# A two-layer transformer trunk on one core: first SwiGLU begun with its 256-column part, x loaded later, and one product order for all down parts

## The chip, the cores and the metric

The kernel runs on one core of a Trainium2 chip. The core has a matrix engine (PE), a vector engine (DVE), an activation engine (ACT), a general engine (POOL) and a sync engine (SP) that issues DMAs. Each engine takes its instructions in the order in which they were queued and waits on semaphores for the others. The metric is device time in microseconds for one execution of the whole program, and the median of several runs is compared.

## What is computed

Two layers, each with a SwiGLU, a token mixer (eight forgetting-attention heads and four differential-attention heads) and a second SwiGLU, all with residuals; then a final RMSNorm. There are 512 tokens, width 1024, inner width 2816, and everything is float32. What matters here is the SwiGLU and the norm at the end:

```python
def _rmsnorm(x, gain):
    x32 = x.astype(jnp.float32)
    y = x32 * lax.rsqrt(jnp.mean(x32 * x32, axis=-1, keepdims=True) + NORM_EPS)
    return (y * gain.astype(jnp.float32)).astype(x.dtype)

def _swiglu(h, w_gate_up, w_down):
    g, u = jnp.split(h @ w_gate_up, 2, axis=-1)
    return (jax.nn.silu(g) * u) @ w_down
...
  x = x + 1/2 * SwiGLU_1(RMSNorm(x))
  x = x + W_out [FoX_heads(h) ; Diff_heads(h)],  h = RMSNorm(x)
  x = x + 1/2 * SwiGLU_2(RMSNorm(x))
```

## The kernel before

**Arithmetic.** Every float32 matmul is three matmuls of a rounded type (`mm3`, lines 389 to 391: high by high, high by low, low by high). So every operand has a high part (a cast by ACT, line 85) and a low part (a subtraction by DVE, line 86). A weight tile is 128 x 1024 (512 KB), is cast into a ring of five slots, and is asked for four units ahead (`ensure`, `next_w`).

**Parts.** A SwiGLU is cut along its 2816 inner columns into six parts (`CHUNKS`): five of 512 and one of 256, the third. Each part has a gate-and-up step ("u") and a down step ("d"); the order is u0, u1, d0, u2, d1, ..., u5, d4, d5. The text calls d5 the last down part.

**Products.** Each step is a 2 x 2 block product done with seven products in place of eight, named "1" to "7". The weight of a product is a block (11, 12, 21, 22) or a sum. "5" (21+22) and "7" (11+21) are made by a load of one block (SP) and an accumulate-DMA of the other onto it (POOL, line 136). The sum for "6" is added by DVE (line 147) from block 11 and the one of "5", and the sum for "3" by DVE (line 151) from block 12 and that of "6". A u product on a 512-column part has 24 matmuls of 512 columns in two weight units; on the 256-column part it has 24 matmuls of 256 columns and one weight unit. A down product has 12 matmuls of 512 columns (6 on the 256-column part). The order of products is `STEADY` = 1562734, except `FIRST` = 1256374 in u0 and `FINAL` = 1265734 in d5. In the first two products of u0 the two token halves are interleaved.

**The forms of x.** Products need x in seven forms (`XFORM`): the blocks of x for "1", "2", "3" and sums for the rest. At the start of the program they are made from the transposed x (`xT`, loaded by line 1204, into `xin`): block forms of the first token half (line 368 and the casts), then `first_forms` (lines 374 to 384) for the second half and the sums, partly on ACT, mostly on DVE; `ws` is their scratch, and the tiles `xf` hold the result.

**Start.** PE runs 18 warm-up matmuls (line 264). `first_rms` sums the squares of xT (ACT 1233, DVE 1235, PE 1238) and the reciprocal root `nst` (line 315) is needed by the silu of part 0 (line 445). `load_x` (line 1243) loads x in its untransposed form, four times 512 KB, which the first down step adds to; `first_consts` loads constants.

**Down steps and hooks.** The results of a down step are added to x by DVE (`upd`, line 515), four [128 x 512] pieces per product pair. PSUM has eight banks; tag "b" has five, tag "a" three. In a down step, a pair of accumulators (`pa`, tag b) is used by products 1, 6, 7 and 4 in turn, another pair of tag b by product 2, and a pair of tag a by 5 and 3. After each product of d5 a hook runs: `to_next` begins the next stage (after "6" the first half of the tokens, k-pairs 0 and 1, is transposed by PE, line 327, and split into the tiles XA by ACT 343 and DVE 344), and in the last SwiGLU `tail` prepares the final norm (POOL multiplies by the gain, line 1143).

Of the kernel before, what the change touches and what calls it, by code (L numbers as in the profile page):

```python
# [46 lines left out]
FINAL = "1265734"  # L47
# [7 lines left out]
def trunk(ctx, tc, xT, x, gains, gain_row, w_gu, w_dn, w_in, w_ff, w_out, fbias, lams, subln, consts, rope, out):  # L55
# [358 lines left out]
    def gate_up(c, order, after):  # L414

        cols = CHUNKS[c]
        units = 2 if cols == 512 else 1
# [12 lines left out]
        def done(q, p):  # L430
            rc, nr = norm["rc"], norm["nr"]
# [114 lines left out]
    def ffn(pieces, x_done):  # L546
# [3 lines left out]
        def turned(c):  # L550
            yf[c] = []
            fs = turn_h(c, hs.pop(c), (("X", 2), ("X", 3)) if c == NCH - 1 else ("y0", "y1"), yf[c])
# [617 lines left out]
    def to_next(prep, first, q):  # L1170
# [182 lines left out]
```

## Time and profile before

| what | value |
|---|---|
| runs before | 1898.7, 1898.39, 1896.07 us |
| median | 1898.39 us |
| profiled execution, its own time | 1896.68 us |
| its span in the trace | 1894.8 us |
| PE busy | 1836.0 us (97% of the span) |
| DVE busy | 1623.8 us (86%) |
| ACT busy | 1142.4 us (60%) |
| granted clock, mean | 0.987 of full |

The profiled execution was 1.7 us quicker than the median, and its span leaves out 1.9 us of its time. PE is busy in nearly all of the span. The places to read are the few where it is not, and those where its granted clock is below 1.00.

### The profile page before, as it was taken

How to read it: one execution, taken by the hardware profiler on the slowest of the kernel's cores; microseconds unless marked ns; L12 is line 12 of the kernel's file. 1: busy time of each engine (PE TensorE's matmuls, PEld its weight loads, DVE VectorE, ACT ScalarE, POOL GpSimd, SP SyncE). 2: the span in 40 equal slices, each digit the busy share in tenths (PEclk: the TensorE clock that was granted, in tenths of full speed). 3: DMA queues.
4: the chain of work that ended last, by engine and by line, in shares of the span. 5: the costliest groups of instructions: out<-in, count | busy, mean ns of one | idle time of the engine just before them, and what ended most of it. 6: DMA issues, size and time to landing. Idle time of an engine off the chain costs nothing.

```text
span 1894.8 us, 24754 instructions
## 1 busy us (share of the span) xinstructions
PE 1836.0 (97%) x8814; PEld 1508.7 (80%) x8814; DVE 1623.8 (86%) x2538; ACT 1142.4 (60%) x1800; POOL 128.6 (7%) x156
## 2 busy tenths in 40 slices
PE   5999999899999999999999999999999999999997
PEld 2888888687877889888778988877788788888885
DVE  7789898978685989899998989997786869998998
ACT  5646556555786755565486556555677957455564
POOL 1000000000000000000001000000000000000101
PEclk7999999999999999999999999999999999999999
DMA  9675675243346576676558666552433367756742
GB/s 293 179 213 148 188 213 151 80 123 112 96 123 194 158 194 177 158 212 181 165 141 234 167 173 181 174 142 95 129 101 108 108 177 198 207 146 187 221 116 85
DMA packets 96107, 305.39 MB, mean 161 GB/s; under 512 B 12632, under 2 KB 15192, under 8 KB 95984
## 3 DMA queue, kind: packets, MB, share of 16 engines
q1 hardware_dynamic: 75104, 232.68, 36.6%
q0 software_dynamic: 19584, 69.21, 20.7%
q10 hardware_dynamic: 1296, 1.93, 0.4%
q8 instruction: 69, 1.13, 0.2%
q14 instruction: 54, 0.44, 0.1%
HBM read 289.03 MB, written 2.16 MB: 154 GB/s over the span
## 4 chain that ended last, share of the span: by engine, by line
PE 82%; DVE 8%; ACT 5%; DMA 2%; issue 1%; SPq 0%; POOL 0%; DVEq 0%; ACTq 0%
PE ps_c L389 12%; PE ps_c L390 12%; PE ps_c L391 11%; PE ps L391 9%; PE ps L389 9%; PE ps L390 9%; PE ps_a L389 3%; PE ps_a L390 3%; PE ps_a L391 3%; DVE wg L86 2%; PE ps_t L486 2%; DVE x L515 2%; DMA raw<-w_gu 1%; PE ps_a L661 1%; PE ps_a L662 1%; PE ps_a L663 1%
## 5 line engine op out<-in xcount | busy, mean ns | idle before, releaser
L85 ACT CAST wg<-raw 128x1024 fp32r<-128x1024 f32 (+1 forms) x534 | 544.7, 1028 | 507.8 <-PE ps L391 178.3
L86 DVE TENSOR_TENSOR wg<-raw,wg 128x1024 fp32r<-128x1024 f32 (+1 forms) x534 | 629.0, 1187 | 119.8 <-ACT wg L85 117.9
L389 PE MATMUL ps_c<-wg,xf 128*128 128x512 f32 (+1 forms) x768 | 287.8, 375 | 19.6 <-ACT wg L85 18.8
L390 PE MATMUL ps_c<-wg,xf 128*128 128x512 f32 (+1 forms) x768 | 286.6, 373 | 4.4 <-DVE wg L86 4.4
L391 PE MATMUL ps_c<-wg,xf 128*128 128x512 f32 (+1 forms) x768 | 285.5, 373 | 0.0
L389 PE MATMUL ps<-wg,xf 128*128 128x512 f32 (+1 forms) x576 | 218.3, 379 | 0.5 <-ACT wg L85 0.5
L390 PE MATMUL ps<-wg,xf 128*128 128x512 f32 (+1 forms) x576 | 214.9, 373 | 0.0
L391 PE MATMUL ps<-wg,xf 128*128 128x512 f32 (+1 forms) x576 | 214.4, 373 | 0.0
L389 PEld LDWEIGHTS ps_c<-wg,xf 128*128 128x128 f32 x768 | 144.9, 189 | 48.3 <-ACT wg L85 20.5
L390 PEld LDWEIGHTS ps_c<-wg,xf 128*128 128x128 f32 x768 | 144.9, 189 | 30.6 <-DVE wg L86 5.9
L391 PEld LDWEIGHTS ps_c<-wg,xf 128*128 128x128 f32 x768 | 145.1, 189 | 25.6 <-DVE xf L86 0.5
L136 POOL DMA_DIRECT2D raw<-w_gu x88 | 76.4, 868 | 1145.7 <-DMA raw<-w_gu 682.6
L389 PE MATMUL ps_c<-wg,hf 128*128 128x512 f32 x352 | 139.2, 396 | 2.4 <-DVE x L515 2.1
L391 PE MATMUL ps_c<-wg,hf 128*128 128x512 f32 x352 | 137.7, 391 | 0.0
L390 PE MATMUL ps_c<-wg,hf 128*128 128x512 f32 x352 | 137.6, 391 | 0.0
L515 DVE SCALAR_TENSOR_TENSOR x<-ps_c,x 128x512 f32<-128x512 f32 x192 | 123.7, 679 | 2.1 <-PE ps_c L391 2.0
L389 PEld LDWEIGHTS ps<-wg,xf 128*128 128x128 f32 x576 | 109.2, 190 | 19.5 <-ACT wg L85 1.4
L391 PEld LDWEIGHTS ps<-wg,xf 128*128 128x128 f32 x576 | 109.0, 189 | 19.2
L390 PEld LDWEIGHTS ps<-wg,xf 128*128 128x128 f32 x576 | 109.3, 190 | 17.9 <-DVE wg L86 0.2
L389 PE MATMUL ps<-wg,hf 128*128 128x512 f32 x264 | 103.7, 394 | 8.1 <-DVE x L515 8.1
L389 PE MATMUL ps_a<-XA,wg 128*128 128x512 f32 x256 | 106.0, 414 | 2.6 <-ACT XA L343 2.6
L390 PE MATMUL ps<-wg,hf 128*128 128x512 f32 x264 | 103.9, 393 | 1.4 <-DVE wg L86 1.4
(275 smaller groups left out, 3514.2 us busy)
## 6 DMA issues: line engine op xcount, KB each, us to landing
raw<-w_gu SPq DMA_DIRECT2D x218, 512.0 KB, 4.6
raw<-w_dn SPq DMA_DIRECT2D x100, 512.0 KB, 3.4
raw<-w_gu POOLq DMA_DIRECT2D x88, 512.0 KB, 7.0
raw<-w_in SPq DMA_DIRECT2D x48, 512.0 KB, 3.5
raw<-w_dn POOLq DMA_DIRECT2D x40, 512.0 KB, 5.5
kdup<-qk_t SPq DMA_DIRECT2D x64, 128.0 KB, 2.4
raw<-w_out SPq DMA_DIRECT2D x16, 512.0 KB, 3.5
raw<-w_dn SPq DMA_DIRECT2D x20, 256.0 KB, 3.2
```

Source lines behind the costliest of these rows:

```text
L85: act.copy(out=hi, in_=src)
L86: dve.tensor_tensor(out=lo, in0=src, in1=rf(hi), op=ALU.subtract)
L136: pool.dma_start(out=t, in_=where(two, h)[1], accum_op=ALU.add)
L389: pe.matmul(p, lh, rh, start=start, stop=False, skip_group_check=again)
L390: pe.matmul(p, lh, rl, start=False, stop=False, skip_group_check=again)
L391: pe.matmul(p, ll, rh, start=False, stop=stop, skip_group_check=again)
L486: pe.transpose(pj[j][:, e * 256 + p * P:e * 256 + (p + 1) * P], hs[j][p][:, o:o + P], ident)
L515: dve.scalar_tensor_tensor(out=xc, in0=src, scalar=scale, in1=xc, op0=ALU.mult, op1=ALU.add)
L661: pe.matmul(pv[t], xh[:, ts], wh[:, sl], start=k == 0, stop=False)
L662: pe.matmul(pv[t], xh[:, ts], wl[:, sl], start=False, stop=False)
L663: pe.matmul(pv[t], xl[:, ts], wh[:, sl], start=False, stop=k == KT - 1)
```

## The change

The first SwiGLU of layer 0 alone is cut as (256, 512, 512, 512, 512, 512); the other three keep their cut. So u0 there has products of 24 half-width matmuls with one weight unit each. The host packs the weights to match. In this u0 the finishing of product "2", which needs the reciprocal root, is done after "6". At the start all four loads of the first token half of xT come ahead of the second weight, and the weight for "2" comes as one load; the loads behind are asked for earlier than the constants; `first_rms` moves from behind product 2 to behind the third product. `load_x` keeps its place in the list of pieces, 6, but u0 now has seven units, so the four loads of x come after the last of them and behind the weight loads asked for until then. `FINAL` is gone: d5 takes `STEADY`, in all four SwiGLUs, and the hooks of product 6 move to 7; in `tail` those of 7 move to 3.

```diff
-CHUNKS = (512, 512, 256, 512, 512, 512)
-COL0 = [sum(CHUNKS[:i]) for i in range(len(CHUNKS))]
+PARTS_OF = [(256, 512, 512, 512, 512, 512)] + [(512, 512, 256, 512, 512, 512)] * (2 * DEPTH - 1)
...
 STEADY = "1562734"
 FIRST = "1256374"
-FINAL = "1265734"
...
     def part_order(kind, c):
-        if kind == "u":
-            return FIRST if c == 0 else STEADY
-        return FINAL if c == NCH - 1 else STEADY
+        return FIRST if (kind, c) == ("u", 0) else STEADY
...
         def done(q, p):
-            rc, nr = norm["rc"], norm["nr"]
...
+            late = {"2": "", "6": "62"} if first and c == 0 else {}
+            for r in late.get(q, q):
+                done_one(r, p)
...
+        def done_one(q, p):
+            rc, nr = norm.get("rc"), norm.get("nr")
...
-        elif q == "6":
+        elif q == "7":
...
                 early_half(t, 0)
-        elif q == "7":
+        elif q == "3":
...
                 early_half(t, 1)
-        elif q == "3":
...
                 sq(t, 0)
...
-        elif q == "6":
+        elif q == "7":
...
                 prep(0, kp, None)
         elif q == "3":
...
     load_xt(0, 0)
     step[0] = 512
     ensure(1)
-    load_xt(0, 1)
+    for kp in range(1, KP):
+        load_xt(0, kp)
+    step[0] = 1024
...
-    step[0] = 1024
-    for kp in (0, 1):
-        prep_forms(0, 0, kp, xf[:, kp, :, 0:256])
-    load_xt(0, 2)
-    load_xt(0, 3)
-    ensure(4)
-    for kp in (2, 3):
+    for kp in range(KP):
         prep_forms(0, 0, kp, xf[:, kp, :, 0:256])
     for kp in range(KP):
         load_xt(1, kp)
+    running.append(True)
+    ensure(3)
...
-    running.append(True)
...
         for kp in kps:
             prep_forms(0, 1, kp, xf[:, kp, :, 256:512])
...
-        acc = t_tile([P, S], F32, "acc", 5)
+        acc = home("y1", [P, S], F32, "acc")
...
     def load_x():
...
-    pieces = {0: [lambda: first_forms((0, 1))], 1: [lambda: first_forms((2, 3)), first_rms], 6: [load_x]}
+    pieces = {0: [lambda: first_forms((0, 1))], 1: [lambda: first_forms((2, 3))], 2: [first_rms], 6: [load_x]}
...
-        ffn(pieces, lambda q, l=l: to_next(plain_, lambda: mixer_loads(l), q))
+        ffn(2 * l, pieces, lambda q, l=l: to_next(plain_, lambda: mixer_loads(l), q))
```

**DVE at the start.** The names: `raw` are loaded weight blocks, `wg` split weights, `xf` the forms. First as it was, from the sums for the last pairs of x on:

```order
L383 SCALAR_TENSOR_TENSOR ws_251<-ws_251 128x256
L86 TENSOR_TENSOR xf2_158<-ws_251,xf2_158 128x512
L384 SCALAR_TENSOR_TENSOR ws_251<-ws_251,bt_155 128x256
L375 SCALAR_TENSOR_TENSOR ws_261<-xin_109,ngains_70,bt_162 128x256
L376 SCALAR_TENSOR_TENSOR ws_261<-xin_109,ngains_70,ws_261 128x256
L383 SCALAR_TENSOR_TENSOR ws_261<-ws_261 128x256
L86 TENSOR_TENSOR xf2_159<-ws_251,xf2_159 128x768
L86 TENSOR_TENSOR wg_190<-raw_187,wg_190 128x1024
L384 SCALAR_TENSOR_TENSOR ws_261<-ws_261,bt_162 128x256
L86 TENSOR_TENSOR wg_236<-raw_193,wg_236 128x1024
L86 TENSOR_TENSOR xf3_165<-ws_261,xf3_165 128x512
L86 TENSOR_TENSOR xf3_166<-ws_261,xf3_166 128x768
```

and now, from the first block sum on:

```order
L145 TENSOR_TENSOR raw_112<-raw_160,raw_112 128x1024
L84 TENSOR_TENSOR wg_163<-raw_160,wg_163 128x1024
L149 TENSOR_TENSOR raw_123<-raw_123,raw_112 128x1024
L84 TENSOR_TENSOR wg_191<-raw_112,wg_191 128x1024
L84 TENSOR_TENSOR xf1_139<-ws_241,xf1_139 128x768
L84 TENSOR_TENSOR wg_200<-raw_123,wg_200 128x1024
L84 TENSOR_TENSOR wg_253<-raw_166,wg_253 128x1024
L372 SCALAR_TENSOR_TENSOR ws_280<-xin_109,ngains_70,ws_280 128x256
L379 SCALAR_TENSOR_TENSOR ws_280<-ws_280 128x256
L84 TENSOR_TENSOR xf2_145<-ws_280,xf2_145 128x512
L380 SCALAR_TENSOR_TENSOR ws_280<-ws_280,bt_142 128x256
L371 SCALAR_TENSOR_TENSOR ws_290<-xin_109,ngains_70,bt_149 128x256
```

The sums of blocks (now line 145, 149) and four weight low parts stand ahead of the forms of the third and fourth k-pair (`xf2`, `xf3`), where they stood behind them.

**ACT at the end of u0.** The table load that follows `nst` belongs to silu; `p1` and `u2` are its operands. As it was:

```order
L315 ACT_TABLE_LOAD
L315 ACTIVATE nst_299<-nst_299 128x4
L85 CAST wg_379<-raw_150 128x1024
L445 ACT_TABLE_LOAD
L445 ACTIVATE p1_321<-p1_321,nst_299 128x512
L445 ACTIVATE p1_329<-p1_329,nst_299 128x512
```

and now:

```order
L311 ACT_TABLE_LOAD
L311 ACTIVATE nst_364<-nst_364 128x4
L83 CAST wg_513<-raw_195 128x1024
L83 CAST wg_529<-raw_171 128x1024
L446 ACT_TABLE_LOAD
L446 ACTIVATE p1_215<-p1_215,nst_364 128x256
L446 ACTIVATE p1_229<-p1_229,nst_364 128x256
L451 ACTIVATE u2_393<-u2_393,nst_364 128x256
L451 ACTIVATE u2_409<-u2_409,nst_364 128x256
```

Two casts of weights of u1 (`wg_513`, `wg_529`) stand between the reciprocal root and the table load for silu, where there was one, of u0's product 4 (`wg_379`). The first of the two takes a ring slot that product 4 of u0 frees.

**DVE at the change from d4 to d5, first SwiGLU.** `upd` is line 515 before, 516 now; `ps_c` are the pairs of pa, `ps_5` and `ps_2` those of products 5/3 and 2. As it was:

```order
L147 TENSOR_TENSOR raw_2567<-raw_2548,raw_2567 128x1024
L515 SCALAR_TENSOR_TENSOR x2_107<-ps_5_2605,x2_107 128x512
L151 TENSOR_TENSOR raw_2610<-raw_2610,raw_2567 128x1024
L86 TENSOR_TENSOR wg_2734<-raw_2567,wg_2734 128x1024
L515 SCALAR_TENSOR_TENSOR x3_108<-ps_5_2606,x3_108 128x512
L86 TENSOR_TENSOR wg_2752<-raw_2548,wg_2752 128x1024
L515 SCALAR_TENSOR_TENSOR x0_105<-ps_c_2583,x0_105 128x512
L515 SCALAR_TENSOR_TENSOR x1_106<-ps_c_2584,x1_106 128x512
L86 TENSOR_TENSOR wg_2771<-raw_2588,wg_2771 128x1024
L515 SCALAR_TENSOR_TENSOR x0_105<-ps_c_2769,x0_105 128x512
L515 SCALAR_TENSOR_TENSOR x1_106<-ps_c_2770,x1_106 128x512
```

and now:

```order
L145 TENSOR_TENSOR raw_2564<-raw_2545,raw_2564 128x1024
L516 SCALAR_TENSOR_TENSOR x2_107<-ps_5_2602,x2_107 128x512
L516 SCALAR_TENSOR_TENSOR x3_108<-ps_5_2603,x3_108 128x512
L84 TENSOR_TENSOR wg_2731<-raw_2564,wg_2731 128x1024
L84 TENSOR_TENSOR wg_2748<-raw_2607,wg_2748 128x1024
L516 SCALAR_TENSOR_TENSOR x0_105<-ps_c_2580,x0_105 128x512
L149 TENSOR_TENSOR raw_2607<-raw_2607,raw_2564 128x1024
L516 SCALAR_TENSOR_TENSOR x1_106<-ps_c_2581,x1_106 128x512
L84 TENSOR_TENSOR wg_2768<-raw_2585,wg_2768 128x1024
L516 SCALAR_TENSOR_TENSOR x0_105<-ps_c_2766,x0_105 128x512
L516 SCALAR_TENSOR_TENSOR x1_106<-ps_c_2767,x1_106 128x512
```

Here `ps_c_2583` (now 2580) is the accumulator of d4's product 4, `ps_5_2605` (now 2602) that of its product 3, and `ps_c_2769` (now 2766) that of d5's product 1. The two updates from product 3 stand together now, ahead of two weight low parts; the sum of line 149 stands between the two from product 4.

## Rows read from the trace of the kernel before

**Rows 1.** The page: busy time of each engine, its share of the span, instructions.
```profile
PE 1836.0 (97%) x8814; PEld 1508.7 (80%) x8814; DVE 1623.8 (86%) x2538; ACT 1142.4 (60%) x1800; POOL 128.6 (7%) x156
```

**Rows 2.** Windows of the start, and of one half-width product; clock stands before DMA share.
```profile
core 0: us, PE busy (x) PEld busy (x) DVE busy (x) ACT busy (x) POOL busy (x), PEclk, DMA share, GB/s
0.00:15.00 15.00, 13.72 (x45) 6.74 (x45) 6.43 (x10) 11.51 (x22) 1.35 (x11) 1.00 0.88 288
15.00:24.00 9.00, 5.10 (x22) 3.86 (x21) 9.00 (x18) 6.73 (x13) 4.70 (x7) 0.98 1.03 355
24.00:46.00 22.00, 4.15 (x8) 2.13 (x8) 17.08 (x23) 10.17 (x13) 0.85 (x1) 0.50 1.01 276
46.00:54.00 8.00, 8.00 (x23) 6.66 (x24) 4.07 (x12) 2.07 (x3) 0.86 (x1) 0.50 0.88 259
55.00:60.00 5.00, 5.00 (x24) 4.14 (x23) 1.23 (x1) 4.97 (x8) 0.00 (x0) 1.00 0.61 163
...
135.60:138.47 2.87, 2.87 (x25) 2.86 (x24) 2.87 (x4) 1.43 (x2) 0.86 (x1) 1.00 0.40 60
```

**Rows 3.** PE's timeline: start, duration, instruction, idle time before it with its releaser.
```profile
38.33 0.79 PE L389 MATMUL ps_c<-wg,xf 128*128 128x512 f32 x1 [18.23 <-ACT wg L85]
...
45.94 0.80 PE L390 MATMUL ps_c<-wg,xf 128*128 128x512 f32 x1 [1.60 <-DVE wg L86]
```

**Rows 4.** Timelines of SP and POOL: loads of x, and the first accumulate-DMA.
```profile
17.39 1.54 SPq L1243 DMA_DIRECT2D x<-x  x3
...
18.53 1.05 POOL L136 DMA_DIRECT2D raw<-w_gu  x1 [0.98 <-DMA raw<-w_gu]
```

**Rows 5.** ACT's timeline: the cast that awaits the first accumulated block, then the end of part 0.
```profile
27.89 1.04 ACT L85 CAST wg<-raw 128x1024 fp32r<-128x1024 f32 x1 [2.74 <-DMA raw<-w_gu]
...
55.52 1.28 ACT L445 ACT_TABLE_LOAD   x1
56.81 1.34 ACT L445 ACTIVATE p<-p,nst 128x512 f32<-128x512 f32 x2
```

**Rows 6.** DVE's timeline, the start: form steps, a block sum (weight low parts last as long).
```profile
24.61 0.47 DVE L376 SCALAR_TENSOR_TENSOR ws<-xin,ngains,ws 128x256 f32<-128x256 f32 x1
...
25.34 0.94 DVE L86 TENSOR_TENSOR xf<-ws,xf 128x768 fp32r<-128x768 f32 x1
...
35.98 1.22 DVE L147 TENSOR_TENSOR raw<-raw 128x1024 f32<-128x1024 f32 x1
```

**Rows 7.** The page's groups with waits in down steps, and the first such wait (PE's timeline).
```profile
L389 PE MATMUL ps_c<-wg,hf 128*128 128x512 f32 x352 | 139.2, 396 | 2.4 <-DVE x L515 2.1
...
L389 PE MATMUL ps<-wg,hf 128*128 128x512 f32 x264 | 103.7, 394 | 8.1 <-DVE x L515 8.1
...
L390 PE MATMUL ps<-wg,hf 128*128 128x512 f32 x264 | 103.9, 393 | 1.4 <-DVE wg L86 1.4
...
352.88 0.50 PE L389 MATMUL ps<-wg,hf 128*128 128x512 f32 x1 [3.01 <-DVE x L515]
```

**Rows 8.** Windows of the first wait, and behind the second and third; columns as Rows 2.
```profile
350.00:355.00 5.00, 1.65 (x6) 1.05 (x6) 5.00 (x7) 1.38 (x3) 0.00 (x0) 1.00 0.00 0
942.00:944.00 2.00, 2.00 (x6) 1.24 (x5) 2.00 (x3) 0.00 (x0) 0.00 (x0) 0.50 0.60 231
944.00:946.00 2.00, 2.00 (x7) 1.59 (x8) 2.00 (x4) 1.05 (x1) 0.86 (x1) 0.69 0.75 262
1280.00:1282.00 2.00, 1.67 (x4) 0.88 (x4) 2.00 (x4) 1.05 (x1) 0.00 (x0) 0.50 0.31 66
```

**Rows 9.** The first mixer's start: a split of XA (ACT), and PE's first projection.
```profile
359.30 0.83 ACT L343 ACTIVATE XA<-ps_t,gains_sb 128x256 fp32r<-128x256 f32 x2
...
372.59 0.50 PE L389 MATMUL ps_a<-XA,wg 128*128 128x512 f32 x1 [0.68 <-ACT XA L343]
```

**Rows 10.** The page, DMA issues: KB each, median us from issue to landing.
```profile
raw<-w_gu POOLq DMA_DIRECT2D x88, 512.0 KB, 7.0
...
raw<-w_dn POOLq DMA_DIRECT2D x40, 512.0 KB, 5.5
```

More of the change, by code (lines that the diff above doesn't have):

```diff
@@ L164, in gu_units @@
     def gu_units(n, c, order, i):
-        groups = 2 if CHUNKS[c] == 512 else 1
-        base = sum(8 if w == 512 else 4 for w in CHUNKS[:c])
+        groups = PARTS_OF[n][c] // 256
+        base = sum(8 if w == 512 else 4 for w in PARTS_OF[n][:c])
         tags = {("11", 0): "R0", ("11", 1): "R1", ("7", 0): "R2", ("22", 0): "V0", ("7", 1): "V1",
@@ L172, in dn_units @@
     def dn_units(n, c, order, i):
-        cols = CHUNKS[c] // 256 * 512
-        base = sum(CHUNKS[:c]) // 256 * 4 * 512
+        cols = PARTS_OF[n][c] // 256 * 512
+        base = sum(PARTS_OF[n][:c]) // 256 * 4 * 512
         tags = {"11": "s2", "7": "R2", "22": "V0", "12": "V3", "5": "s0"}
@@ L200, in plain @@
         return tag, 3, need, make
-    NCH = len(CHUNKS)
+    NCH = len(PARTS_OF[0])
     PARTS = [("u", 0)]
@@ L412, in banks, with gate_up @@
         return [psum(tag, name) for p in range(2)]
-    def gate_up(c, order, after):
-        cols = CHUNKS[c]
-        units = 2 if cols == 512 else 1
+    def gate_up(cols, first, c, order, after):
+        units = cols // 256
         own = {}
@@ L474, in gate_up, with turn_h @@
         return hs
-    def turn_h(c, hs, where, yf):
+    def turn_h(cols, hs, where, yf):
         out_ = []
-        for kp in range(CHUNKS[c] // 256):
+        for kp in range(cols // 256):
             def one(kp=kp):
@@ L507, in turn_h, with down @@
         return out_
-    def down(c, order, after, yf, x_done):
+    def down(order, after, yf, x_done):
         pa, own = banks("b", "ps_c"), {}
-        kps = CHUNKS[c] // 256
+        kps = len(yf)
         def upd(t, half, src, scale):
@@ L544, in down, with ffn @@
             x_done(q)
-    def ffn(pieces, x_done):
+    def ffn(n, pieces, x_done):
         hs, yf = {}, {}
@@ L551, in turned @@
             yf[c] = []
[L552 removed]
+            fs = turn_h(PARTS_OF[n][c], hs.pop(c), (("X", 2), ("X", 3)) if c == NCH - 1 else ("y0", "y1"), yf[c])
             return {1 + i: [f] for i, f in enumerate(fs)}
@@ L556, in ffn @@
             if kind == "u":
-                hs[c] = gate_up(c, order, pieces if c == 0 else turned(c - 1))
+                hs[c] = gate_up(PARTS_OF[n][c], n == 0, c, order, pieces if c == 0 else turned(c - 1))
             else:
                 after = turned(NCH - 1) if c == NCH - 2 else {}
-                down(c, order, after, yf.pop(c), x_done if c == NCH - 1 else lambda q: None)
+                down(order, after, yf.pop(c), x_done if c == NCH - 1 else lambda q: None)
     side = {}
@@ L1306 @@
         for j in (1, 2):
+            chunks = PARTS_OF[2 * l + j - 1]
+            col0 = [sum(chunks[:i]) for i in range(len(chunks))]
             wg, wd = a[f"ffn{j}_w_gate_up"][l], a[f"ffn{j}_w_down"][l]
             parts = []
-            for c0, w in zip(COL0, CHUNKS):
+            for c0, w in zip(col0, chunks):
                 b = blocks(np.stack([wg[:, c0:c0 + w], wg[:, FF + c0:FF + c0 + w]], 1), w)
@@ L1315 @@
             parts = []
-            for c0, w in zip(COL0, CHUNKS):
+            for c0, w in zip(col0, chunks):
                 for m in blocks(wd[c0:c0 + w].reshape(w, 2, S), S):
```

4 lines of the change are left out of this document (2 added, 2 removed).

## The prediction

> **What bounds the kernel now.** I read the page first. PE is busy for 97% of the span [rows 1], so most of the 1894.8 us can't move: the change keeps the number of matmul columns in every SwiGLU. What can move is PE's idle time and the time in which its clock is granted at half. The windows show where that is. Between 24 and 46 us PE has 4.15 of 22.00 us busy at a clock of 0.50, while the DMA share is 1.01; from 46 to 54 us it is busy throughout, still at 0.50 [rows 2]. PE's timeline names the wait: 18.23 us for a weight cast, ending at 38.33 us, and continuous work only from 45.94 us [rows 3]. That cast waits for blocks which the accumulate-DMAs finish: the first was issued at 18.53 us [rows 4] and its cast began at 27.89 us [rows 5]. The second place is the end of every SwiGLU. The page's groups give 8.1 us of waits for `upd` in matmuls into `ps`, 2.1 us in `ps_c`, 1.4 us for a low part [rows 7]. In the first such wait, 3.01 us long [rows 7], DVE is busy for all of 350 to 355 us [rows 8]: it isn't waiting itself, the update stands behind other work in its queue.
>
> **Start: how far ahead part 0 comes.** By 54 us before, PE has done 48 matmuls of two products, 8 between 24 and 46 us, and 15 between 46 and 54 us (23, of which 8 are the narrow ones of the square sum) [rows 2]: 71 of 512 columns, the work of 142 half-width ones. Full clock is there from 55 us [rows 2]. In the new u0, six products are 144 half-width matmuls, 2.87 us for 24 at full clock [rows 2]. So I compare 55 us with the time at which six products end.
>
> The block that "5" is accumulated on is now the fourth weight load instead of the seventh, and the constants come behind it: some 1.3 MB less ahead of it, at 288 to 355 GB/s [rows 2] 3.7 to 4.5 us. I take 3.9, since most of it falls in the faster window. The accumulate is issued at 18.5 - 3.9 = 14.6 us. From issue to cast it took 27.89 - 18.53 = 9.4 us in this stretch [rows 4, 5]; the median over the program is 7.0 us [rows 10]. So the block is there between 21.6 and 24.0 us; I take 23.4, near the row of the same stretch, a little less since x's loads (issued at 17.39 us [rows 4]) no longer share the bandwidth. From there on DVE's queue sets the time: two block sums, five weight low parts, seven form steps and five form low parts stand in a row (the order above shows the first twelve). Of an instruction's time some 0.09 us lies under the next one, so a sum or weight low part counts 1.13 us, a step about 0.37, a form low part 0.60 or 0.87 [rows 6]: 7 x 1.13 + 7 x 0.37 + 3 x 0.87 + 2 x 0.60 = 14.3 us. The last form, 0.87 of it, isn't needed at once: PE, which works in part from 24.5 us on, is continuous from about 23.4 + 14.0 = 37.4 us, where before it was so from 45.94 us [rows 3].
>
> PE then has 94 of the 144 matmuls behind it by my walk through its queue, and 50 left. At full clock they take 6.0 us, ending at 43.4. Before, the clock rose 8 to 9 us after continuous work began [rows 2, 3]; if so again, it is at half until about 46 us, and the six products end at 47.5. The lead is 55 minus these: **7.6 to 11.7 us**, middle 9.6.
>
> **Start: what is given back.** At the end of u0 two casts of u1's weights stand on ACT ahead of the table load and the four silu halves, and the first of them waits for the ring slot of product 4. Behind that wait stand silu, DVE's products with it, and the transposes that PE meets 0.9 us into u1. After product 4: two casts of 1.04, a table load of 1.28 [rows 5], four activations of about 0.35 (half of the 0.67 that one takes in rows 5), two DVE steps of 0.4 [rows 6] = 5.6 us less overlaps, say 4.4 to 5.2; less 0.9 this is a stall of 3.5 to 4.3 us that the kernel before doesn't have. I take 4.0. A fall of the clock behind it would cost 1.6 us (below). **Net 5.6 us**, from 9.6 - 4.0; its ends are 7.6 - 4.3 - 1.6 = 1.7 and 11.7 - 3.5 = 8.2. The moved x loads cost nothing: the first down step comes after u1, some 40 us later, and 2 MB take 7 us at 276 GB/s [rows 2].
>
> **Last down parts.** In `FINAL` product 2 comes second, and its bank is one that d4's product 4 frees only by its updates; on DVE these stand behind a block sum and two low parts. In `STEADY` product 5 comes second: its bank is freed by d4's product 3, one product earlier, whose updates now stand together. Product 5 so puts 12 matmuls, 2.7 us, between. What is late next is product 6: it writes the bank that `upd` of product 1 must have read. From the end of d4's product 4, PE has about 22 matmuls (5.0 us) until there. DVE has four updates of 0.60, a block sum and a low part (4.7 us), and one or two low parts of backlog, 1.1 to 2.3: a stall of 0.8 to 1.9; I take 1.3 at the three boundaries and 0.8 at the end.
>
> The waits removed are 8.1 + 2.1 + 1.4 = 11.6 us [rows 7]. Two of them are followed by half clock: 942 to 944 at 0.50 and 944 to 946 at 0.69 lose 1.0 + 0.6 us, and 1280 to 1282 at 0.50 loses 1.0 [rows 8]; I count these 2.6 us as returned. That is 14.2 - 3 x 1.3 - 0.8 = **9.5 us**. Bounds: 11.6 - 4 x 1.9 = 4.0 without the clock, 14.2 - 4 x 0.3 = 13 with stalls nearly hidden.
>
> The Trainium skill (TensorE: Matmul & The Clock Gate, "What's actually happening") says that half rate is the default and that activity releases the full rate. The first stall, longest of all, has 1.00 in its window [rows 8], so this trace doesn't tie a fall to each stall. Were it so for each, the stalls that stay would cost 1.6 us more apiece; the sum leaves that out.
>
> **Hooks.** The half-0 splits of XA now begin two products (5.4 us) later. The first was at 359.30 us, PE's first use at 372.59 us, and that matmul waited 0.68 us for a split of ACT [rows 9]. Thirteen us of cover become eight, so nothing should be late for PE; but the splits of ACT (0.42 each) now lie in the stretch in which ACT is the last. Bounds: none, or four splits, 1.7 us, at three places. I take **1.0 us lost** in all.
>
> **Sum.** 5.6 + 9.5 - 1.0 = 14.1 us. The profiled execution took 1896.7 us; less this, 1882.6. The median of the runs was 1.7 us higher, so I put the new median at 1884 us, a ratio of 0.992. A measurement of this kernel can tell 0.2%, 3.8 us, from no change.
>
> **Rivals.**
> 1. *The start gives nothing.* The clock stays at half through the patchy work, and the stall at the hand-over brings it down again: 1.7 us or less. For it: the whole stretch from 24 to 54 us was at 0.50 [rows 2], and PE's early work is now shorter, with pauses. Against it: the 3.9 us come from the order of loads alone. 1898.4 - 0 to 2 - 8.5 gives about 1889.
> 2. *The stalls only move.* DVE is busy all through the first boundary [rows 8]; if it is the bound over d4 and d5, another product waits for what product 2 awaited. Only the start remains: 1898.4 - 5.6 + 0 to 1 = 1893. Against it: the 8.1 us are three waits in all, one in each of the first three d5; d0 to d4 run in `STEADY` and have none.
> 3. *Slower: the hook comes too late.* If the first use of XA at the three boundaries waits for the moved splits in full, each costs up to 5.4 us, 16 us in all, and the kernel ends at about 1900. It decides from about 4.7 us at each boundary (14.1 / 3), which needs all of the cover of 8 us gone. Against it: XA's first half was split 10 us ahead of its use [rows 9].
> 4. *Accumulates are quick.* If they land after 5.5 us, as those of the down weights do [rows 10], "5" is there at 20.1 us instead of 23.4; with an early clock the time is 1884 - 3.3 - 2 = 1878. The Trainium skill (DMA: Bandwidth & Descriptors, "Anatomy of one DMA") fits 2.0 us plus bytes by 436 GB/s, which for 512 KB is 3.2 us, and 2 us less again. The trace doesn't agree: 9.4 us here, since other loads share the engines.
> 5. *The change doesn't do what it says.* The bytes ahead of the sixth product are the same and DMA is the bound (share 1.01 [rows 2]), so part 0 ends as before and the stall is added: with the down parts, 1898.4 + 4 - 8.5 = 1894.
>
> **Chances.** The forecast 0.50 (1878 to 1889 as its own range), rival 1 0.18, rival 2 0.10, rival 3 0.05, rival 4 0.12, rival 5 0.05. The range leaves out rival 3 and the ends of 4: 1873 to 1894. Faster by over 0.2% means under 1894.6: the forecast, rivals 1 and 4, and most of 2 and 5: 0.88. Within 0.2%: 0.08. Slower: 0.04.
>
> **What would show it.** Right: PE continuous from 36 to 39 us; the first accumulate issued at 14 to 15 us; a PE wait of 3 to 5 us for transposed part 0 right after u0; in the last down parts waits of about 1 us, at product 6, instead of 3; the end of the span 10 us behind the last update, as before. Wrong: a first accumulated cast after 26 us, or a clock of 0.50 beyond 50 us (start); waits over 2 us for `upd` at d5 (last down parts); first projections that wait more than 2 us for XA (hooks).

## The result

The changed kernel takes 1886.87 us (median of four runs, 1885.72 to 1887.99), the kernel before 1897.36 us in the same comparison (1896.07 to 1898.70). The ratio is 0.9945, with a 95% interval of 0.9927 to 0.9962: 10.5 us faster. The forecast was 14 us, 1884 us, with a range of 1873 to 1894.

Both traces hold 8814 matmul records of PE, so the same-numbered records can be compared: the shift of a record is its start after less its start before. (In the first SwiGLU the parts have another order, so the shift is read there only behind the part where both have done the same columns.)

| record of PE | before, us | after, us | shift, us |
|---|---|---|---|
| 1040, first SwiGLU, behind the start | 244.05 | 238.87 | -5.2 |
| 1430, ahead of its last down part | 329.91 | 324.80 | -5.1 |
| 1608, first projection of mixer 1 | 372.59 | 364.84 | -7.7 |
| 1950, inside mixer 1 | 448.50 | 443.01 | -5.5 |
| 4160, second SwiGLU | 900.19 | 894.75 | -5.4 |
| 4420, end of its last down part | 960.08 | 951.44 | -8.6 |
| 4560, first part of the third SwiGLU | 993.74 | 986.76 | -7.0 |
| 5850, ahead of its last down part | 1259.09 | 1252.11 | -7.0 |
| 5980, end of that | 1291.71 | 1282.02 | -9.7 |
| 6500, inside mixer 2 | 1402.75 | 1395.37 | -7.4 |
| 8580, ahead of the last down part of all | 1829.93 | 1821.54 | -8.4 |
| end of the span | 1894.84 | 1885.18 | -9.7 |

The table tells the story. The start is worth 5.2 us. Each of the next three last down parts gains 2.6 to 3.2 us, and the stage behind it gives 1.7 to 2.3 of them back. The last one gains 1.3 us. Another 1.0 us appears inside mixer 2 (records 6500 to 7150). Some 0.3 us of it lie where the trace before has a granted clock of 0.72 (1494 to 1500 us) and the trace after 1.00. Some 0.7 us lie at records 7070 to 7100; other kernels below gain them too, with the old order (e4) or the new one (e5, e7), and others with the new order don't (e2, e6, e8), so they don't go with the change.

### The profile page after: what moved, and what is told of

It reads as the page before. It is cut to its first block, busy times and chain, and to the rows that moved or that the text cites. A ratio compares the mean times of both kernels' runs of the same rounds, so it can differ in the third digit from the quotient of the medians.

```text
span 1885.2 us, 24722 instructions
## 1 busy us (share of the span) xinstructions
PE 1837.5 (97%) x8814; PEld 1511.2 (80%) x8814; DVE 1625.6 (86%) x2537; ACT 1139.6 (60%) x1797; POOL 129.0 (7%) x156
## 3 DMA queue, kind: packets, MB, share of 16 engines
q8 instruction: 69, 1.13, 0.2%
## 4 chain that ended last, share of the span: by engine, by line
PE 81%; DVE 10%; ACT 5%; DMA 2%; issue 1%; SPq 0%; DVEq 0%; ACTq 0%
PE ps_c L385 12%; PE ps_c L386 12%; PE ps_c L387 12%; PE ps L386 9%; PE ps L385 9%; PE ps L387 9%; PE ps_a L385 3%; PE ps_a L386 3%; PE ps_a L387 3%; DVE wg L84 3%; PE ps_t L487 2%; DVE x L516 1%; ACT pg L859 1%; DMA raw<-w_gu 1%; PE ps_b L871 1%
## 5 line engine op out<-in xcount | busy, mean ns | idle before, releaser
L385 PE MATMUL ps_a<-XA,wg 128*128 128x512 f32 x256 | 106.9, 418 | 2.6 <-ACT XA L339 1.9
L386 PE MATMUL ps_a<-XA,wg 128*128 128x512 f32 x256 | 101.9, 398 | 2.5 <-DVE XA L340 2.5
L386 PE MATMUL ps<-wg,hf 128*128 128x512 f32 x264 | 103.2, 391 | 0.0
```

The source lines that it names most:

```text
L385: pe.matmul(p, lh, rh, start=start, stop=False, skip_group_check=again)
L386: pe.matmul(p, lh, rl, start=False, stop=False, skip_group_check=again)
```

## The profile after

The start in windows (columns as in [rows 2]):

```profile
core 0: us, PE busy (x) PEld busy (x) DVE busy (x) ACT busy (x) POOL busy (x), PEclk, DMA share, GB/s
24.00:30.00 6.00, 5.39 (x23) 5.09 (x24) 6.00 (x7) 4.85 (x6) 2.72 (x4) 0.50 1.01 307
30.00:34.00 4.00, 2.12 (x13) 1.70 (x11) 4.00 (x9) 1.35 (x2) 1.70 (x2) 0.90 0.90 225
34.00:38.00 4.00, 4.00 (x21) 3.70 (x20) 4.00 (x6) 2.43 (x4) 0.00 (x0) 0.57 1.04 254
38.00:46.00 8.00, 8.00 (x58) 7.54 (x57) 7.16 (x13) 6.62 (x10) 0.86 (x1) 1.00 1.04 352
46.00:54.00 8.00, 6.73 (x45) 5.82 (x43) 6.80 (x14) 2.71 (x5) 0.00 (x0) 1.00 1.00 335
54.00:56.00 2.00, 0.00 (x0) 0.00 (x0) 1.67 (x4) 1.99 (x4) 0.86 (x1) 0.67 0.29 115
56.00:60.00 4.00, 3.78 (x13) 3.36 (x14) 3.52 (x6) 4.00 (x9) 0.88 (x1) 0.50 0.93 122
60.00:62.00 2.00, 2.00 (x7) 1.52 (x7) 2.00 (x6) 0.02 (x1) 0.00 (x0) 0.63 0.81 160
62.00:66.00 4.00, 4.00 (x19) 3.30 (x18) 2.57 (x3) 3.37 (x5) 0.00 (x0) 1.00 0.34 126
```

From 30 us on PE works where it idled before [rows 2, 3], and from 38 to 54 us it has the full clock, which it had before only from 55 us. But in 54 to 56 us it is idle, and then its clock is 0.50 again until about 61.5 us. The rows behind that, of POOL, ACT and PE in turn (start, duration, instruction, idle time before it with its releaser):

```profile
15.07 1.05 POOL L134 DMA_DIRECT2D raw<-w_gu  x1 [11.18 <-DMA raw<-w_gu]
...
22.88 1.04 ACT L83 CAST wg<-raw 128x1024 fp32r<-128x1024 f32 x1 [3.22 <-DMA raw<-w_gu]
...
51.84 1.99 ACT L83 CAST wg<-raw 128x1024 fp32r<-128x1024 f32 x2 [4.20 <-PE ps_c L387]
53.85 1.28 ACT L446 ACT_TABLE_LOAD   x1
...
33.52 0.39 PE L385 MATMUL ps_c<-wg,xf 128*128 128x256 f32 x1 [0.69 <-ACT xf L83]
...
43.16 0.28 PE L387 MATMUL ps_c<-wg,xf 128*128 128x256 f32 x1
43.28 0.40 PE L385 MATMUL ps_c<-wg,xf 128*128 128x512 f32 x1
...
48.78 0.28 PE L385 MATMUL ps_c<-wg,xf 128*128 128x256 f32 x1
...
56.22 0.48 PE L487 MATMUL ps_t<-ident,p 128*128 128x128 f32 x1 [3.49 <-DVE p L453]
```

The first accumulate is issued at 15.07 us (before at 18.53 [rows 4]) and its block is cast at 22.88 (before 27.89 [rows 5]). PE's last wait of the start ends at 33.52 us. The 144th half-width matmul, the last of six products, begins at 43.16 us. PE then takes matmuls of u1 (512 columns, until 48.8 us), and only from 48.78 us the half-width product 4. ACT waits 4.20 us for the ring slot that this product frees, at 51.84 us, and only behind two casts of u1's weights, at 53.85 us, comes the table load for silu. PE meets the transposes of part 0 and waits 3.49 us, until 56.22.

The groups of the page that answer to [rows 1] and [rows 7]:

```profile
PE 1837.5 (97%) x8814; PEld 1511.2 (80%) x8814; DVE 1625.6 (86%) x2537; ACT 1139.6 (60%) x1797; POOL 129.0 (7%) x156
...
L385 PE MATMUL ps_c<-wg,hf 128*128 128x512 f32 x352 | 138.6, 394 | 4.4 <-DVE x L516 4.3
...
L386 PE MATMUL ps_a<-XA,wg 128*128 128x512 f32 x256 | 101.9, 398 | 2.5 <-DVE XA L340 2.5
```

The group with 8.1 us of waits for `upd` (matmuls into `ps`) is gone; the waits for `upd` in `ps_c` grew from 2.1 to 4.3 us. In PE's timeline they stand, with what comes behind each:

```profile
350.37 0.47 PE L385 MATMUL ps_c<-wg,hf 128*128 128x512 f32 x1 [1.35 <-DVE x L516]
...
364.84 0.50 PE L385 MATMUL ps_a<-XA,wg 128*128 128x512 f32 x1 [0.64 <-ACT XA L339]
...
371.15 0.50 PE L386 MATMUL ps_a<-XA,wg 128*128 128x512 f32 x1 [1.23 <-DVE XA L340]
...
938.37 0.47 PE L385 MATMUL ps_c<-wg,hf 128*128 128x512 f32 x1 [0.81 <-DVE x L516]
...
972.41 0.73 PE L385 MATMUL ps_c<-wg,xf 128*128 128x512 f32 x2 [1.29 <-ACT wg L83]
...
974.16 0.50 PE L386 MATMUL ps_c<-wg,xf 128*128 128x512 f32 x1 [1.02 <-DVE wg L84]
...
978.46 0.50 PE L386 MATMUL ps_c<-wg,xf 128*128 128x512 f32 x1 [0.81 <-DVE wg L84]
...
1274.18 0.47 PE L385 MATMUL ps_c<-wg,hf 128*128 128x512 f32 x1 [1.04 <-DVE x L516]
...
1863.13 0.47 PE L385 MATMUL ps_c<-wg,hf 128*128 128x512 f32 x1 [0.82 <-DVE x L516]
```

The last down parts now wait 1.35, 0.81, 1.04 and 0.82 us, where the longest waits were 3.01, 2.48, 2.65 and 1.40 us. The waits behind them grew instead: in mixer 1 PE waits 0.64 us for ACT's split of XA, as before [rows 9], and then 1.23 us for DVE's, where it was 0.60 us for ACT's; at 972 to 979 us, in the first part of the third SwiGLU, it waits 1.29, 1.02 and 0.81 us for casts and low parts of weights, 3.1 us in place of 1.2. The windows at the first two boundaries have the full clock; behind the third (last line) it falls to half from about 1297 to 1300.5 us, where the trace before has 1.00:

```profile
346.00:356.00 10.00, 8.65 (x39) 6.81 (x38) 10.00 (x14) 3.16 (x3) 0.00 (x0) 1.00 0.16 52
366.00:376.00 10.00, 8.43 (x35) 5.72 (x34) 7.52 (x24) 9.94 (x23) 0.00 (x0) 1.00 0.22 77
955.00:965.00 10.00, 10.00 (x49) 8.10 (x48) 9.99 (x17) 9.91 (x20) 0.00 (x0) 1.00 0.01 2
1295.00:1305.00 10.00, 9.95 (x32) 7.17 (x33) 4.91 (x16) 6.16 (x12) 0.00 (x0) 0.83 0.31 107
```

DVE is busy for 10.00 of 10.00 us in the last down part, and ACT for 9.94 of 10.00 behind it. Before, ACT was as busy there: 9.94 of 10.00 us from 372 to 382 us, where the first projections then stood.

## The experiments

The times below are differences from the kernel before, measured on the same chip in the same comparison; the changed kernel stands at -10.5 us. Its own interval reaches from -13.9 to -7.2 us, and the kernels below have intervals of 3 to 6 us, so two times that lie 3 us or less apart don't tell two kernels apart by themselves. The traces, from which the shifts are read, are of one execution each. A diff is against the changed kernel unless its sentence names another.

**Each half of the change alone (e1, e2).** First the start without the new order of d5 and its hooks:

```diff
+FINAL = "1265734"
...
-        return FIRST if (kind, c) == ("u", 0) else STEADY
+        if kind == "u":
+            return FIRST if c == 0 else STEADY
+        return FINAL if c == NCH - 1 else STEADY
...
-        elif q == "7":
+        elif q == "6":
...
-        elif q == "3":
+        elif q == "7":
...
+        elif q == "3":
...
-        elif q == "7":
+        elif q == "6":
```

> The changed kernel with the down parts as before: d5 takes FINAL again and the hooks stand at 6 and 7; only the new cut, the late x and the new order of loads are left. Theory (parts add up, the shift between the traces is 5.1 us from 160 us on): 5 us faster than before, about 1892. Rival (the start and the down parts act on each other, the gain of the whole change is the start's): 9 to 10 us faster, about 1887.5.

1893.50 against 1898.51 us, ratio 0.9974 (0.9965 to 0.9983): **-5.0 us**. Then the new order of d5 and the hooks, in the kernel before:

```diff
-        return FINAL if c == NCH - 1 else STEADY
+        return STEADY
...
-        elif q == "6":
+        elif q == "7":
...
-        elif q == "7":
+        elif q == "3":
...
-        elif q == "3":
...
-        elif q == "6":
+        elif q == "7":
```

> The kernel before with only the product order of d5 changed to STEADY and the hooks moved to 7 and 3. Theory (the stalls of the down parts go, some 9.7 us, but the stage behind each boundary gives most of it back): 4 to 5 us faster than before, about 1893. Rival (the forecast's term: 9.5 us less 1.0 for the hooks): 8.5 us faster, about 1889. Second rival (the stalls only move): 0 to 1 us.

1892.86 against 1898.51 us, ratio 0.9974 (0.9963 to 0.9986): **-5.7 us**. The halves add up to 10.7, the whole is 10.5: within what the intervals tell, they don't act on each other. The down parts bring two thirds of the forecast's 8.5 us, so neither rival holds as put: the stalls go, and a good part comes back.

**Is it the late hook (e4)?** The forecast's only cost behind the boundaries was the hook that moved by two products. Here it is moved in the kernel before, and the order of products stays:

```diff
-        elif q == "6":
+        elif q == "7":
...
-        elif q == "7":
+        elif q == "3":
...
-        elif q == "3":
...
-        elif q == "6":
+        elif q == "7":
```

> The kernel before, its product order FINAL kept, with only the hooks moved to 7 and 3. If the give-back at the three boundaries comes from the late hook: 1.4 to 2.3 us at each, 4 to 6 us slower than before, about 1902. If it comes from elsewhere (the order of products, or casts of weights that were late anyway): within 1 us of before.

1895.77 against 1898.51 us, ratio 0.9987 (0.9978 to 0.9996): **-2.7 us**, faster if anything. The late hook by itself costs nothing, and this theory fell. It isn't without effect, though: in this trace the longest waits of the first three last down parts are 1.89, 1.43 and 1.64 us instead of 3.01, 2.48 and 2.65, with the old order of products, and behind them the shift falls back by 0.9, 3.4 (with a half clock from 979 to 986 us) and 1.0 us. So a part of what d5 gains comes from the hook's work having left it, and that work stands behind d5 instead.

**Is it the half of x that is ready later (e5)?** In `STEADY` product 2 comes fourth, and the first half of x is complete only behind it. Here product 2 and with it the hook stand third, as early as the hook stood before.

```diff
+LAST = "1526734"
...
-        return FIRST if (kind, c) == ("u", 0) else STEADY
+        if kind == "u":
+            return FIRST if c == 0 else STEADY
+        return LAST if c == NCH - 1 else STEADY
...
-        elif q == "7":
+        elif q == "2":
...
-        elif q == "3":
+        elif q == "7":
...
+        elif q == "3":
...
-        elif q == "7":
+        elif q == "2":
```

> The changed kernel with d5 in the order 1526734: product 5 stays second, product 2 comes third, so the first half of the tokens 0 and 1 is complete one product earlier, and the hook stands behind 2. If what is given back behind the boundaries hangs on when that half of x is ready: 3 to 4 us faster than the changed kernel, about 1883. If it is ACT's and DVE's weight work: as the changed kernel, 1886 to 1888. If product 2's bank stalls again: 1 to 2 us at each boundary, about 1891.

1888.78 against 1898.51 us, ratio 0.9952 (0.9939 to 0.9964): **-9.7 us**, as the changed kernel. Between the same records as in the table the shift falls back by 0.9, 2.1 and 1.8 us behind its last down parts. This one fell as well, and the late hook with the new order of products, too.

**Is it DVE's work (e7)?** Two block sums of 1.13 us each leave DVE at each boundary:

```diff
-    def forms(order, groups, cols, where, ring0):
+    def forms(order, groups, cols, where, ring0, bare=False):
...
-                dve.tensor_tensor(out=src, in0=get("5", h), in1=src, op=ALU.add)
+                if not bare:
+                    dve.tensor_tensor(out=src, in0=get("5", h), in1=src, op=ALU.add)
...
-            if f in "26" and ("2", h) in seen and ("6", h) in seen:
+            if not bare and f in "26" and ("2", h) in seen and ("6", h) in seen:
...
-        return forms(order, 1, cols, where, i)
+        return forms(order, 1, cols, where, i, c == NCH - 1)
```

> The changed kernel without the two block sums on DVE (for the weights of 6 and 3) in the last down parts; these weights are then single blocks, so that part of the computation is left out. It takes 2.3 us of DVE's work from each of the four boundaries. Theory (what is given back behind the boundaries hangs on DVE, which is busy throughout): 1.5 to 2.3 us less at each, 5 to 8 us faster than the changed kernel, about 1880. Rival (it hangs on ACT's squares and splits of x): the waits in d5 shrink by 1 us each, but the next stage starts as late: 0 to 2 us faster.

1881.77 against 1898.71 us, ratio 0.9907 (0.9893 to 0.9922): **-16.9 us**, 6.4 us more than the changed kernel. So of the 9.0 us that are taken from DVE, 6.4 come through. In the trace, which is of the quickest of its five executions (1878.26 us), the net gains of the four boundaries (what d5 gains, less what is given back behind it) are 3.1, 3.4, 2.8 and 2.9 us, where the changed kernel has 0.4, 1.5, 0.4 and 1.3. They come in d5 itself: its longer waits for `upd` are gone, and the first three last down parts gain 4.9, 4.5 and 4.4 us instead of 2.6, 3.2 and 2.7. What is given back behind them stays at 1.8, 1.2 and 1.6 us; in mixer 1 PE now waits for ACT's splits of XA, 0.69, 0.36 and 0.96 us. So DVE's queue sets the pace from d4 to the end of d5. Behind it there are waits that less work of DVE in d5 doesn't take away.

**Or ACT's (e8)?** Behind d5, squares of x stand among the splits of XA on ACT, as the changed kernel's timeline shows:

```profile
365.05 1.05 ACT L303 ACTIVATE sq<-x 128x1024 f32<-128x1024 f32 x1
...
366.09 1.56 ACT L339 ACTIVATE XA<-ps_t,gains_sb 128x256 fp32r<-128x256 f32 x4
```

```diff
-    def squares(half):
+    def squares(half, bare=False):
...
-        for t in (2 * half, 2 * half + 1):
+        if bare and half == 0:
+            pool.memset(norm["ss"], 1024.0)
+        for t in () if bare else (2 * half, 2 * half + 1):
...
-    def sums():
-        squares(0)
-        squares(1)
+    def sums(bare=False):
+        squares(0, bare)
+        squares(1, bare)
...
-            sums()
+            sums(True)
```

> The changed kernel with the sums of squares of x left out at the two mixers (a constant stands for them), which takes 5.3 us of ACT's work from the stretch between d5 and the first projections. Theory that ACT is the last there: the 2 us given back at each mixer's start stay, 3 to 4.5 us faster than the changed kernel, about 1883. Theory that DVE is: within 1 us of it.

1885.55 against 1898.71 us, ratio 0.9930 (0.9917 to 0.9943): **-13.2 us**, 2.7 us more than the changed kernel, but the two intervals overlap. The trace has the second wait of mixer 1 at nearly its length:

```profile
370.16 0.49 PE L388 MATMUL ps_a<-XA,wg 128*128 128x512 f32 x1 [1.01 <-DVE XA L342]
```

1.01 us here, 1.23 in the changed kernel, and 0.64 us for the first wait in both. The net gains at the two mixers are 1.5 and 2.0 us, instead of 0.4 and 0.4, but the changed kernel's second one contains the half clock of 1297 to 1300.5 us, which this execution doesn't have, and a kernel that keeps the squares (e12) gains 1.5 us at the first mixer as well. So it isn't shown that ACT's squares have a part; this run also took the square root and its table load out of the stretch.

**The hand-over from u0 to u1 (e6).** The two casts of u1's weights that stand ahead of silu, and the next one, are held back behind it:

```diff
-    ready, running = [], []
+    ready, running, norm = [], [], {}
...
-            ready.append((tag, make()))
+            if 11 <= pos[0] - 1 <= 13 and "mark" in norm:
+                with tc.issue_after(norm["mark"].ins):
+                    ready.append((tag, make()))
+            else:
+                ready.append((tag, make()))
...
-
-    norm = {}
```

> The changed kernel with the three casts of u1's weights that stood ahead of silu on ACT (wg_513, wg_529 and the next) held back behind the silu of part 0. Theory (the hand-over from u0 to u1 costs a PE wait of 3.5 us and then some 3 us of half clock): 5 to 6.5 us faster than the changed kernel, about 1881. Rival (PE waits for the held-back casts instead, or the clock falls anyway): within 1.5 us of the changed kernel.

1881.66 against 1898.71 us, ratio 0.9907 (0.9893 to 0.9922): **-17.1 us**, 6.6 us more than the changed kernel, and nothing is left out: the best version of this study. PE's wait for the transposes, and windows of this run:

```profile
51.95 0.33 PE L489 MATMUL ps_t<-ident,p 128*128 128x128 f32 x1 [0.45 <-DVE p L455]
...
48.00:52.00 4.00, 3.55 (x27) 3.02 (x26) 3.56 (x11) 1.13 (x3) 0.00 (x0) 1.00 1.03 416
52.00:56.00 4.00, 4.00 (x22) 3.38 (x23) 3.45 (x5) 4.00 (x8) 0.43 (x1) 1.00 0.58 227
56.00:60.00 4.00, 4.00 (x20) 3.30 (x19) 3.79 (x7) 4.00 (x6) 1.30 (x2) 1.00 0.71 88
60.00:66.00 6.00, 6.00 (x28) 4.99 (x27) 6.00 (x6) 4.74 (x7) 0.00 (x0) 1.00 0.66 165
```

The wait is 0.45 us in place of 3.49, and the clock stays at 1.00. The changed kernel paid the wait and the half clock behind it. The shift of record 1040 is -12.1 us instead of -5.2: 3.0 us of the wait, 2.6 of the half clock, and 1.2 which this execution has ahead of the hand-over already (its 144th half-width matmul begins at 41.92 us).

**Late x (e9).** The four loads of x where they were before, beside the accumulates:

```diff
+    for t in range(NB):
+        sp.dma_start(out=xs[t], in_=x[t * P:(t + 1) * P, :])
...
-    def load_x():
-        for t in range(NB):
-            sp.dma_start(out=xs[t], in_=x[t * P:(t + 1) * P, :])
-    pieces = {0: [lambda: first_forms((0, 1))], 1: [lambda: first_forms((2, 3))], 2: [first_rms], 6: [load_x]}
+    pieces = {0: [lambda: first_forms((0, 1))], 1: [lambda: first_forms((2, 3))], 2: [first_rms]}
```

> The changed kernel with the four loads of x right behind the constants, ahead of the weights of u1 and beside the accumulates, as they were in the kernel before. Theory (late x only keeps the bandwidth free, 0.6 us at the first accumulates): up to 1.5 us slower than the changed kernel. Rival (the 2 MB push back what PE waits for, 7 us of DMA): 4 to 7 us slower, so that the start's whole gain is the late x.

1888.72 against 1898.71 us, ratio 0.9945 (0.9932 to 0.9958): **-10.0 us**. The two times don't tell the kernels apart. In the trace the 144th half-width matmul begins at 44.56 us instead of 43.16, and the shift of record 1040 is -3.7 instead of -5.2. So the late load of x is worth no more than some 1.5 us, as the theory has it, and not the rival's 4 to 7.

**The order of the first loads (e12).** 1.3 MB again ahead of the block for product 5:

```diff
+    first_consts()
+    for t in (0, 1):
+        sp.dma_start(out=xs[t], in_=x[t * P:(t + 1) * P, :])
...
-    first_consts()
...
-        for t in range(NB):
+        for t in (2, 3):
```

> The changed kernel with the constants and two of the loads of x, 1.3 MB, ahead of the block that 5 is accumulated on: what the new order of loads took away stands there again. Theory (the first accumulate sets the start): it is issued 3.9 us later, near 19 us, PE is continuous some 4 us later, and the time is 3 to 5 us above the changed kernel, about 1891, unless the clock rises at another time. Rival (the gain is the half-width part alone): within 1.5 us of the changed kernel.

1888.56 against 1897.59 us, ratio 0.9951 (0.9937 to 0.9964): **-9.0 us**. This is 1.5 us short of the changed kernel, between theory and rival and inside the noise, so the time decides nothing. POOL, PE and DVE in this run, and two windows of it (columns as in [rows 2]):

```profile
18.89 1.05 POOL L134 DMA_DIRECT2D raw<-w_gu  x1 [3.28 <-DMA raw<-w_gu]
...
29.41 0.80 PE L385 MATMUL ps<-wg,xf 128*128 128x256 f32 x2 [11.42 <-ACT wg L83]
...
33.51 0.80 PE L385 MATMUL ps_c<-wg,xf 128*128 128x256 f32 x2 [3.31 <-ACT wg L83]
...
47.46 0.28 PE L387 MATMUL ps_c<-wg,xf 128*128 128x256 f32 x1
...
59.26 0.33 PE L487 MATMUL ps_t<-ident,p 128*128 128x128 f32 x1 [2.14 <-DVE p L453]
...
24.17 0.95 DVE L84 TENSOR_TENSOR xf<-ws,xf 128x768 fp32r<-128x768 f32 x1
25.04 0.42 DVE L380 SCALAR_TENSOR_TENSOR ws<-ws,bt 128x256 f32<-128x256 f32 x1
25.37 0.69 DVE L84 TENSOR_TENSOR xf<-ws,xf 128x512 fp32r<-128x512 f32 x1
28.31 1.23 DVE L145 TENSOR_TENSOR raw<-raw 128x1024 f32<-128x1024 f32 x1 [2.26 <-DMA raw<-w_gu]
...
60.00:62.00 2.00, 2.00 (x10) 1.72 (x9) 1.55 (x3) 2.00 (x4) 0.88 (x1) 0.54 0.91 135
62.00:64.00 2.00, 2.00 (x7) 1.62 (x6) 1.97 (x5) 1.06 (x3) 0.00 (x0) 0.61 1.01 135
```

The first accumulate is issued at 18.89 us, 3.8 later than in the changed kernel, and PE begins the third product at 29.41 us instead of 23.98. It is continuous from 33.51 us in both, since DVE, while it waited for the block, made forms of x (0.95, 0.42, 0.69 us, until 26 us) that stand behind the sums in the changed kernel. But by 33.5 us it has begun 50 half-width matmuls here and 78 there, and the last matmul of the six products, the 144th, begins at 47.46 us instead of 43.16. So the theory's 4 us are there, as 4.3 us of the lead. The hand-over then takes less: product 4 begins 4.3 us behind the 144th matmul instead of 5.6, the wait for the transposes is 2.14 us instead of 3.49, and the half clock behind it loses 0.9 + 0.8 = 1.7 us instead of 2.6. That is 2.2 us less, and the shift of record 1040 is -3.0 instead of -5.2.

**The sums on POOL (e10).** In the version with silu first (the diff is against that), DVE is relieved without leaving anything out:

```diff
-    def forms(order, groups, cols, where, ring0):
+    def forms(order, groups, cols, where, ring0, eng=None):
+        eng = eng or dve
...
-                dve.tensor_tensor(out=src, in0=get("5", h), in1=src, op=ALU.add)
+                eng.tensor_tensor(out=src, in0=get("5", h), in1=src, op=ALU.add)
...
-                dve.tensor_tensor(out=raw["12", h], in0=raw["12", h], in1=raw["11", h], op=ALU.add)
+                eng.tensor_tensor(out=raw["12", h], in0=raw["12", h], in1=raw["11", h], op=ALU.add)
...
-        return forms(order, 1, cols, where, i)
+        return forms(order, 1, cols, where, i, pool if c == NCH - 1 else dve)
```

> The kernel with silu first (1881.7 us in its run), and the two block sums of the last down parts done by POOL in place of DVE; nothing is left out. If the 2.3 us of DVE at each boundary are what is given back (as the run without the sums says, some 5 us in all): 3 to 5 us faster than with silu first, about 1877.5. If POOL's slower sum (its product of 128x512 takes 1.6 us in the trace of before, so some 3.3 us here) makes the weights of 6 and 3 late: 0 to 3 us slower than with silu first.

1883.39 against 1897.59 us, ratio 0.9921 (0.9906 to 0.9935): **-14.2 us**, 2.9 us short of silu first alone; the intervals of the two overlap, but a gain of 3 to 5 us isn't there. The weights aren't late: in the last down parts PE waits for none of them. The trace shows what takes the gain away:

```profile
329.67 2.40 POOL L146 TENSOR_TENSOR raw<-raw 128x1024 f32<-128x1024 f32 x1 [7.48 <-ACT wfs L626]
340.00 2.40 POOL L150 TENSOR_TENSOR raw<-raw 128x1024 f32<-128x1024 f32 x1 [7.94 <-issue]
...
330.43 2.45 DVE L84 TENSOR_TENSOR hf<-ws,hf 128x768 fp32r<-128x768 f32 x1 [0.99 <-ACT hf L83]
...
336.33 1.21 DVE L84 TENSOR_TENSOR wg<-raw,wg 128x1024 fp32r<-128x1024 f32 x1
...
341.00 2.49 DVE L84 TENSOR_TENSOR wg<-raw,wg 128x1024 fp32r<-128x1024 f32 x1
```

POOL's sums run from 329.67 and 340.00 us for 2.40 us each. The DVE instruction that runs beside each takes 2.45 and 2.49 us, where its like takes 0.94 [rows 6] and 1.21. At the other three boundaries it is the same: POOL's sums take 2.40 to 2.91 us, and a low part of DVE beside each takes 2.23 to 2.62 us. DVE loses 1.0 to 1.5 us to each sum that it was to be spared 1.13 us of, 9.8 us in all against 9.0. The rest of the 2.9 us isn't explained; this execution has a half clock behind the third boundary (1293 to 1297 us) that the other lacks.

## Why the prediction was right, and where it was not

**The lead of part 0** was forecast step by step, and the steps held: the accumulate issued at 14.6 us (15.07), the block there at 23.4 (22.88), 94 matmuls behind PE at 37.4 us (96 at 37.46), six products done at 43.4 us if the clock rises early (the last one's last matmul begins at 43.16). The range of 7.6 to 11.7 us took the middle; the measured lead is 54.52 - 43.16 = 11.4 us, between the 72nd matmul of 512 columns before and the 144th of 256 after. It lies near the upper end because the clock was full from 37.6 to 54.7 us. Two details were off. The sum on DVE's queue gives 23.4 + 14.3 - 0.9 = 36.8 us and not 37.4, and PE's last wait ended at 33.52 us already, ahead of the 36 to 39 that were named as a sign. The 3.9 us for the order of loads held: e12 puts 4.3 us of the lead on it. The other 7 us belong to the half-width part and to what else changed at the start; no run took these apart.

**What is given back at u1** was put at 4.0 us: a wait of 3.5 to 4.3, with the half clock named but left out of the sum. The wait was 3.49 us. The half clock came: PE ran 3.78 of the 4 us from 56 us at 0.50 and 2.00 us at 0.63, which loses 1.9 + 0.7 = 2.6 us. Together 6.1, and 11.4 - 6.1 = 5.3 us, as the shift of 5.2 says. The forecast of 5.6 came out right by luck, from a lead 1.8 us too small and a give-back 2.1 us too small. A clock of 0.50 beyond 50 us, which the prediction named as a sign of being wrong, was there from 54.7 to 61.5 us. e6 shows that the give-back was to be had.

**The stalls of the last down parts** were to bring 9.5 us. The shift falls by 2.6, 3.2 and 2.7 us over the three boundaries and by 1.3 at the end, together 9.8, and the waits that stay, 0.81 to 1.35 us, are near the 0.8 to 1.3 taken. The half clock in the second and third last down part went with them (the third fall lasted from 1279.7 to 1283.2 us and lost 1.5 us, not 1.0). This step held in size; that the hook's move has a share in it (e4) wasn't foreseen.

**The hooks** are the step that failed: 1.0 us was taken for what the stages behind give back, with bounds of up to 1.7 at three places. Measured are 2.3 (records 1608 to 1950), 1.7 (4420 to 4560) and 2.3 us (5980 to 6500), 6.3 in all. It isn't the late hook as such (e4, e5), nor when x's half is ready (e5). What the traces show in its place: PE waits longer for the splits of XA at each mixer (2.2 us instead of 1.5) and for casts and low parts at the second boundary (3.1 instead of 1.2); a wait of 0.62 us for a tile of mixer 1 appears at 417.67 us; and behind the third boundary the half clock loses 1.7 us (9.95 us busy at 0.83). In traces of the same last down parts without that fall (e6, e9, e12) the third place gives back 0.7 to 1.5 us. So a part of the give-back is the clock's. What sets the waits, DVE's work or ACT's, stays open: e7 shows that DVE is the pace up to the end of d5, and e8 doesn't separate ACT. That is rival 2 in part, at a chance of 0.10. It was argued down because PE waits at few matmuls, but few waits don't mean slack on DVE: 5.00 of 5.00 us busy [rows 8] was the row to trust, and the forecast used it for the first wait only. The sum with the measured sizes: 5.2 + 9.8 - 6.3 = 8.7, and 1.0 in mixer 2: 9.7 us, the difference of the two spans.

**The rest.** The moved x costs nothing, as said, and may bring some 1.5 us at the start (e9). The hooks in the tail cost nothing that shows: the end moved with PE. Rivals 1, 3, 4 and 5 did not come about; of rival 1 the fall of the clock at the hand-over did.

## What to carry to other kernels

When a wait of the matrix engine is on an engine that is itself busy throughout, removing the wait may gain only until the next place where that engine is needed: add up its work over the whole stretch, not up to the wait. A part that starts earlier brings the next hand-over earlier too; look at what stands ahead of its first dependent instruction in each queue, because a cast that waits for a ring slot can hold up everything behind it. A cheap test of the first is to leave the suspected work out and see whether the time follows.

## What was not expected of the hardware

A sum of two 128x1024 tiles on POOL took 2.40 to 2.91 us and held up a low part of DVE beside it: 2.45 and 2.49 us at the first boundary, instead of 0.94 and 1.21. These two ended 0.8 and 1.1 us after POOL's sums, about their own length. Updates of x, which read PSUM, ran beside the same sums at their usual 0.67 us. The Trainium skill (SBUF — State Buffer, "SBUF: two separate sides") says that a POOL instruction and a DVE instruction with two SBUF inputs lock the same pair of ports, which the one that starts first holds for its whole length while the other blocks. The low parts, which read two tiles in SBUF, agree with it, and so do the updates, which read one there.

A wait of PE of 3.49 us was followed by some 5 us at half clock after 56 us, one of 3.01 us in the kernel before by none [rows 7, 8], and one of 2.48 us, which ended at 941.36 us in the kernel before, by half clock from 942 to 944 us [rows 8]:

```profile
941.36 0.50 PE L389 MATMUL ps<-wg,hf 128*128 128x512 f32 x1 [2.48 <-DVE x L515]
```

In the kernel after, one of 1.24 us, which ended at 1295.01 us, was followed by half clock from about 1297 to 1300.5 us. The length of the wait alone doesn't tell which it is.
